# Hybrid encoder block on one core: copies of the meta tokens split before the transposes, another order of a pair's products, weights' parts first when few are ready

## The chip, the cores and the metric

One core of a Trainium2 chip runs one launch of the kernel. The metric is the device time of a launch in microseconds (us). Before the change three runs gave 1146.08, 1146.79 and 1147.39 us; the median is 1146.79 us.

## What is computed

One layer of an encoder on 272 tokens (256 tokens and 16 meta tokens) with 2048 features, all in fp32. The reference, cut to what matters:

```python
hn = rmsnorm(h, mix_norm_g)
q_a, k_a, v_a, cq, ckv, k_pe = split(hn @ w_in)             # 8 heads of 128; ranks 512, 256; 64
out_a = neighbourhood_attention(rmsnorm(q_a), rmsnorm(k_a), v_a, rpb, meta_bias)     # "NA"
q  = rmsnorm(rmsnorm(cq) @ w_q_up)                          # 8 heads of 128 + 64 (rotary)
k, v = split(rmsnorm(ckv) @ w_kv_up)                        # 8 heads of 128 each; k joined with k_pe
out_b = softmax(rope(q) @ rope(rmsnorm(k)).T * scale) @ v   # "MLA"
h = h + concat([rmsnorm(out_a), rmsnorm(out_b)]) @ w_out
h = h + (silu(conv3(hn2 @ w_gate)) * (hn2 @ w_up)) @ w_down # hn2 = rmsnorm(h); 2048 -> 5632 -> 2048
```

## The kernel before

**Three products for one.** Each fp32 operand is split into a high part in the format fp32r (a copy by ScalarE, ACT) and a low part, operand minus high part (a subtraction by VectorE, DVE). A product is hi·hi + hi·lo + lo·hi: three matmuls of a 128x128 block of weights with some 260 columns of tokens (`mm3`, lines 381 to 383), or two in the MLP (`mm2`, lines 1407 and 1408). Nearly all time of TensorE (PE) goes there.

**Weights.** They come in pieces of up to 1024 columns in the order of the list `pieces` (lines 295 to 314). SP loads a piece into one of 5 buffers `raw`; ACT makes `whi` from it (`split_hi`, line 339) and DVE `wlo` (`split_lo`, line 348), 512 columns at a time, into 3 buffers each. PE uses the pieces strictly in order and frees them (`used`). Below, such a half piece of 512 columns in `whi` or `wlo` is a weights' part.

**Attention, by pairs of heads.** After the first projections (cq, ckv, the rotary key) there are four pairs (line 1308). A pair has six stages on PE, in this order: NA queries; the MLA products by `w_q_up` (queries), then by `w_kv_up` (keys and values; `up`, line 1270); NA keys; NA values. What ACT, DVE and POOL (GpSimd) do with the results runs beside the next stages: norms, scores, softmax (`na_tile`, `mla_tile`, `na_small`, `mla_small`), the transposes of the probabilities `p`, and the product with the values (`attend`, line 754).

**The copies of the meta tokens.** The 272 keys are two chunks of 128 and one of 16. For the last chunk all three products are made in one matmul: `p` and the values hold the 16 columns three times, 32 columns apart, behind column 272. In `normalized` (line 739) one DVE instruction scales columns 0 to 255 of `p`, another writes the scaled last 16 columns three times (48 columns). The transposes (`chunks_transposed`, line 719) turn 128, 128 and 80 columns into a PSUM bank. `split_chunks` (line 728) then makes on ACT the high part of the first two chunks, on DVE their low part, on ACT the high part of the third (80 rows), and on DVE the low part of 16 rows of it (`split_last`, line 734). After that the bank is free again; there are two banks for transposes.

**What sets the order.** The kernel is written as generators; a planner, `Flow` (line 83), runs them at build time. A generator asks for an engine with a cost in ns; of those that are ready `run` takes the one with the earliest start, then the lowest `prio`, then the first made. The order of each engine's instructions is fixed by this; on the chip the engines only wait for each other's semaphores. Attention work has `prio` 0, PE's main line 1, the splits of the weights 2 (line 1439). `TO_PE`, 700 ns, is put between another engine's result and PE's use of it.

The two lines that set the choice before:

```python
start = max(self.clock[eng], th.t + self.latency(th, eng))
key = (start, th.prio, th.seq)
```

Of the kernel before, what the change touches and what calls it, by code (L numbers as in the profile page):

```python
# [9 lines left out]
F32 = mybir.dt.float32  # L10
# [32 lines left out]


# [3 lines left out]
LP = L + 3 * CW  # L48
# [32 lines left out]


class Flow:
# [94 lines left out]
def encoder_block(ctx: ExitStack, tc: tile.TileContext, io):  # L178
# [61 lines left out]
    def cost(l, r):  # L240
# [3 lines left out]
        return 0.422 * n + 2 if n >= 256 else max(0.84 * n, 1.67 * m, 27)  # L244
# [53 lines left out]
    for i in range(3):  # L298
        add(io["w_in"][i])
    for pr in range(4):  # L300
# [37 lines left out]

    def split_hi():
        for p in pieces:  # L340
            yield p.loaded
            p.hi = yield from one(his)
            for j, ev in enumerate(p.half):
                a, b = 512 * j, min(512 * j + 512, p.n)
                yield from ACT(p.hi[:, a:b], p.raw[:, a:b], AF.Copy)
                fl.set(ev)

    def split_lo():
        for p in pieces:
            p.lo = yield from one(los)  # L350
            for j, ev in enumerate(p.half):
# [5 lines left out]
                fl.set(p.ready[j])  # L357
            fl.put(raws, p.raw)
# [19 lines left out]
    def mm3(ps, xhi, xlo, start, stop):  # L378
        whi, wlo = yield from block()
        yield "pe", 3 * (0.422 * size(xhi) + 2)  # L380
# [338 lines left out]
    def chunks_transposed(t, pt):  # L719

        yield from TR(
            [(pt[:, :P], t[:, :P]), (pt[:, P : 2 * P], t[:, P:SEQ]), last_transposed(t, pt)]
        )

    def last_transposed(t, pt):
        return pt[:KP, 2 * P : 3 * P], t[:, L : L + KP]
# [7 lines left out]
    def split_last(out, src, lo):  # L734
        yield from ACT(out[:KP], src[:KP], AF.Copy)
        e = slice(lo * CW, lo * CW + N_META)
        yield from TT(out[e], src[e], out[e].bitcast(F32), ALU.subtract)

    def normalized(p, w, a, n=P):

        out, src = thrice(p)
        if a < SEQ:
            yield from TS(p[:n, a:SEQ], p[:n, a:SEQ], w, None, ALU.mult)
        yield from TS(out[:n], src[:n], w, None, ALU.mult)

    def p_transposed(p, PT, q0):
# [4 lines left out]
        yield from split_chunks(PT[:, :, q0 : q0 + P], src, 1)  # L751
# [53 lines left out]
    def small_softmax(p, w, a, b):  # L805
# [4 lines left out]
        yield from normalized(p, w[:4, 2:3], a, 4)  # L810
        fl.put(cols, w)

    def split_small(PT, a, pt):

        for c in range(2):
            o = PT[:, c, :, SEQ:NT]
            src = pt[:, : 3 * P].rearrange("p (c q) -> p c q", c=3)[:, :, 2 * c : 2 * c + 2]
            if a == 0:
                yield from split_chunks(o, src, 1)
            else:  # L820
                yield from split_last(o[:, 2], src[:, 2], 1)
# [70 lines left out]
    def na_values(s, c, ps):  # L892
# [3 lines left out]
        yield from TT(vs[:, :SEQ], ps[:, :SEQ], s1[:, :SEQ], ALU.mult)  # L896
        yield from TT(
            thrice(vs)[0], repeated(ps[:, SEQ:L], 3), repeated(s1[:, SEQ:], 3), ALU.mult
        )
        fl.put(acc, ps)  # L900
        pt = yield from one(tps)
# [3 lines left out]
        yield from split_chunks(V, pt[:, : 3 * P].rearrange("p (c d) -> p c d", c=3), 2)  # L905
# [3 lines left out]
    def na_tile(s, c, i, B, PT, done):  # L909
# [18 lines left out]
        yield from normalized(p, w[:, 2:3], 0)  # L928
        fl.put(cols, w)
        yield from p_transposed(p, PT[:, c], q0)  # L930
        fl.set(done)

    def na_small(s, pr, PT, done):
# [19 lines left out]
        yield from TR([last_transposed(p, pt)])  # L953
# [148 lines left out]
    def mla_tile(s, c, i, PT, done):  # L1102
# [19 lines left out]
        yield from normalized(p, w[:, 2:3], 0)  # L1122
        fl.put(cols, w)
        yield from p_transposed(p, PT[:, c], q0)
# [136 lines left out]
    def attention_weights():  # L1261
# [8 lines left out]
        def up(pr):  # L1270
            s = mla_pair(pr)
# [317 lines left out]
```

## Time and profile before

| | |
|---|---|
| runs before (us) | 1146.08, 1146.79, 1147.39 |
| the profiled execution (us) | 1147.3 |
| its span, first to last instruction (us) | 1145.3 |
| PE busy | 1130.8 us (99%), 8072 matmuls |
| DVE busy | 826.2 us (72%), 1777 instructions |
| ACT busy | 659.1 us (58%), 1466 instructions |
| POOL busy | 118.3 us (10%), 158 instructions |
| first projections and the pairs | to about 291 us of the span, the last pair's rest to 313 us |
| output projection | about 291 to 395 us; then the MLP to the end |

Times of the trace count from the span's first instruction. A matmul's record is longer than the step to the next one (its end is modelled, and matmuls overlap), so that idle time before a matmul is shorter than what is lost. A row of a timeline is: start, duration, engine, line, operation, output<-inputs by the program's names, shapes, count; in brackets the idle time of the engine before it and what ended it. A row of a group is: line, engine, operation, names, shapes, count | busy us, mean ns of one | idle us of the engine before them and what ended it.

### The profile page before, as it was taken

The page shows a single profiled execution, that of the slowest core. Times are in us where ns is not written, and L with a number is a line of the kernel's source. Part 1 is how long each engine was busy: PE and PEld are TensorE (multiplying, and loading weights), DVE is VectorE, ACT ScalarE, POOL GpSimd, SP SyncE. Part 2 cuts the span into 40 slices and gives each one's busy share as a digit, 9 for nine tenths or more (in the row PEclk, how much of TensorE's full clock was granted, in tenths as well). Part 3 has the DMA queues.
Part 4 walks back from the last instruction along what each step waited for, and adds up shares of the span by engine and source line. Part 5 has one row for each costly group of instructions (what it writes and reads, how often), then busy time and mean ns, then how long its engine had stood idle before and what let it go on. Part 6 is the DMA issues. An engine that isn't in the chain of part 4 may idle for free.

```text
span 1145.3 us, 21863 instructions
## 1 busy us (share of the span) xinstructions
PE 1130.8 (99%) x8072; PEld 1064.0 (93%) x8072; DVE 826.2 (72%) x1777; ACT 659.1 (58%) x1466; POOL 118.3 (10%) x158
## 2 busy tenths in 40 slices
PE   8999999999899999999999999999999999999998
PEld 8999999999899999999999999999999888888888
DVE  8779898989977867677667767776777655555553
ACT  7677877878645655555555555555555544444442
POOL 0010202020133510001001000100010000000000
PEclk9999999999999999999999999999999999999999
DMA  9544434443465556555555555555556566766662
GB/s 315 187 137 135 139 120 149 135 152 130 146 196 177 184 180 198 188 188 180 188 186 185 184 185 188 180 190 186 190 178 193 173 193 208 209 198 193 199 195 74
DMA packets 63059, 203.62 MB, mean 178 GB/s; under 512 B 6888, under 2 KB 13416, under 8 KB 62952
## 3 DMA queue, kind: packets, MB, share of 16 engines
q1 hardware_dynamic: 62808, 202.11, 54.9%
q8 instruction: 63, 1.03, 0.4%
q14 instruction: 44, 0.36, 0.1%
q10 hardware_dynamic: 144, 0.12, 0.0%
HBM read 200.10 MB, written 2.10 MB: 177 GB/s over the span
## 4 chain that ended last, share of the span: by engine, by line
PE 87%; DVE 6%; ACT 5%; issue 1%; DMA 1%; POOL 0%; SPq 0%; POOLq 0%; ACTq 0%
PE bank L1407 27%; PE bank L1408 14%; PE bank L383 14%; PE bank L382 14%; PE bank L381 14%; PE bank L250 2%; DVE wlo L214 2%; ACT scr L210 1%; DVE scr L222 1%; ACT whi L210 1%; PE bank L256 1%; ACT bank L210 1%; DVE pt L214 1%; DVE p L218 1%; DMA scr<-in_xT 1%
## 5 line engine op out<-in xcount | busy, mean ns | idle before, releaser
L214 DVE TENSOR_TENSOR wlo<-raw,whi 128x512 fp32r<-128x512 f32 (+1 forms) x737 | 519.4, 714 | 251.8 <-ACT whi L210 248.6
L210 ACT ACTIVATE whi<-raw 128x512 fp32r<-128x512 f32 (+1 forms) x737 | 458.8, 629 | 393.6 <-PE bank L1407 174.7
L381 PE MATMUL bank<-hl,whi 128*128 128x258 f32 (+1 forms) x1232 | 356.8, 290 | 1.8 <-ACT whi L210 1.6
L383 PE MATMUL bank<-hl,wlo 128*128 128x258 f32 (+1 forms) x1232 | 350.6, 285 | 3.6 <-DVE wlo L214 3.6
L382 PE MATMUL bank<-hl,whi 128*128 128x258 f32 (+1 forms) x1232 | 351.1, 285 | 0.0
L1407 PE MATMUL bank<-hl,whi 128*128 128x512 f32 x704 | 246.3, 392 | 0.0
L383 PEld LDWEIGHTS bank<-hl,wlo 128*128 128x128 f32 x1232 | 235.1, 191 | 5.2 <-DVE wlo L214 5.1
L381 PEld LDWEIGHTS bank<-hl,whi 128*128 128x128 f32 x1232 | 232.8, 189 | 4.0 <-ACT whi L210 2.9
L382 PEld LDWEIGHTS bank<-hl,whi 128*128 128x128 f32 x1232 | 234.3, 190 | 0.2
L1407 PE MATMUL bank<-act,whi 128*128 128x512 f32 x660 | 228.8, 391 | 0.0
L1408 PE MATMUL bank<-hl,wlo 128*128 128x256 f32 x704 | 197.5, 281 | 0.0
L1408 PE MATMUL bank<-act,wlo 128*128 128x256 f32 x660 | 184.8, 280 | 0.0
L1407 PEld LDWEIGHTS bank<-hl,whi 128*128 128x128 f32 x704 | 132.0, 188 | 28.9
L1407 PEld LDWEIGHTS bank<-act,whi 128*128 128x128 f32 x660 | 123.4, 187 | 27.1
L1408 PEld LDWEIGHTS bank<-hl,wlo 128*128 128x128 f32 x704 | 132.7, 188 | 0.0
L1408 PEld LDWEIGHTS bank<-act,wlo 128*128 128x128 f32 x660 | 124.7, 189 | 0.0
L238 POOL TENSOR_TENSOR mt<-mt,s 128x256 f32<-128x256 f32 x44 | 41.6, 966 | 459.5 <-ACT mt L210 459.5
L222 DVE SCALAR_TENSOR_TENSOR mt<-mt,vecs,mt 128x256 f32<-128x256 f32 x88 | 40.3, 479 | 0.0
L210 ACT ACTIVATE pt<-bank 128x256 fp32r<-128x256 f32 (+3 forms) x88 | 23.7, 281 | 27.1 <-DVE pt L214 20.0
L381 PE MATMUL bank<-ob,whi 128*128 128x258 f32 x128 | 36.7, 286 | 0.0
L382 PE MATMUL bank<-ob,whi 128*128 128x258 f32 x128 | 36.4, 285 | 0.0
L210 ACT ACTIVATE scr<-scr 128x272 f32<-128x272 f32 x77 | 32.0, 424 | 7.4 <-DVE scr L222 6.3
(216 smaller groups left out, 1220.5 us busy)
## 6 DMA issues: line engine op xcount, KB each, us to landing
raw<-in_w_gate SPq DMA_DIRECT2D x88, 512.0 KB, 4.2
raw<-in_w_up SPq DMA_DIRECT2D x88, 512.0 KB, 4.3
raw<-in_w_down SPq DMA_DIRECT2D x80, 512.0 KB, 4.4
raw<-in_w_in SPq DMA_DIRECT2D x54, 512.0 KB, 4.3
raw<-in_w_out SPq DMA_DIRECT2D x32, 512.0 KB, 4.2
raw<-in_w_down SPq DMA_DIRECT2D x16, 256.0 KB, 3.4
raw<-in_w_cq SPq DMA_DIRECT2D x7, 512.0 KB, 5.9
bias<-in_na_bias SPq DMA_DIRECT2D x8, 272.0 KB, 4.0
```

What stands on the lines that cost most here:

```text
L210: nc.scalar.activation(out, in_, f, **kw)
L214: nc.vector.tensor_tensor(out, a, b, op)
L218: nc.vector.tensor_scalar(out, a, s0, s1, *ops)
L222: nc.vector.scalar_tensor_tensor(out, a, s, b, op0, op1)
L238: nc.gpsimd.tensor_tensor(out, a, b, op)
L250: nc.tensor.matmul(o, l, r, start=start, stop=stop)
L256: nc.tensor.transpose(o, i, ident[:n, :n])
L381: nc.tensor.matmul(ps, whi, xhi, start=start, stop=False)
L382: nc.tensor.matmul(ps, whi, xlo, start=False, stop=False)
L383: nc.tensor.matmul(ps, wlo, xhi, start=False, stop=stop)
L1407: nc.tensor.matmul(ps, whi, x, start=start, stop=False)
L1408: nc.tensor.matmul(ps[:, :n], wlo, x[:, 0, :], start=False, stop=stop)
```

## The change

1. **Copies.** `normalized` and `thrice` go. `p` is scaled in one instruction (272 columns), and the values likewise. The new `meta_copies` copies the 16 columns twice on ACT (32 columns, as high parts) and makes the low part by a subtraction on POOL (16 columns), ahead of the transposes. The third transpose takes 128 columns. `split_chunks` makes the high part of all three chunks in one ACT instruction of 384 columns, and on DVE the low part of the first two; the subtraction of 16 rows on DVE is gone.
2. **Order of a pair's stages**: `ORDER = "QKqkVv"` (capitals MLA, small letters NA). The pieces follow it: `w_kv_up` is loaded as two pieces of 512 columns.
3. **Weights' parts**: `prio` of `split_hi` and `split_lo` is -1 instead of 2 while, after the first 16 pieces, fewer than two pieces beyond PE's place have been split.
4. Costs of matmuls in the planner are larger (0.445 ns a column and 3 for 0.422 and 2; `mm2` 347 for 325). A small copy in `small_sums` goes from POOL to DVE.

```diff
+ORDER = "QKqkVv"
-LP = L + 3 * CW
+LP = L + P
...
-        if th.eng == eng and (eng == "pe" or th.prio >= 2):
+        if th.eng == eng and (eng == "pe" or callable(th.prio) or th.prio >= 2):
...
-                key = (start, th.prio, th.seq)
+                key = (start, th.order(), th.seq)
...
-        return 0.422 * n + 2 if n >= 256 else max(0.84 * n, 1.67 * m, 27)
+        return 0.445 * n + 3 if n >= 256 else max(0.84 * n, 0.84 * m, 27)
...
-    def thrice(row):
+    def meta_copies(row, lo, n=P):
 
-        out = row[:, L : L + 3 * CW].rearrange("p (i x) -> p i x", i=3)[:, :, :N_META]
-        return out, repeated(row[:, SEQ:L], 3)
+        out = row[:n, L : L + 3 * CW].rearrange("p (i x) -> p i x", i=3)[:, :, :N_META]
+        src = row[:n, SEQ:L]
+        his = out[:, :2] if lo == 2 else out[:, ::2]
+        yield from ACT(his.bitcast(F32R), repeated(src, 2), AF.Copy)
+        yield from PTT(out[:, lo].bitcast(F32R), src, out[:, 0], ALU.subtract)
...
     for pr in range(4):
-        for i in range(6):
-            if i == 2:
+        for stage in ORDER:
+            if stage == "Q":
                 add(io["w_q_up"][pr])
-                add(io["w_kv_up"][pr])
-            add(io["w_in"][3 + 6 * pr + i])
+            elif stage in "KV":
+                o = 512 * (stage == "V")
+                add(io["w_kv_up"][pr][:, o : o + 512])
+            else:
+                add(io["w_in"][n_in])
+                add(io["w_in"][n_in + 1])
+                n_in += 2
...
-    def split_chunks(out, src, lo):
+    def split_chunks(out, src):
 
-        yield from ACT(out[:, 0:2], src[:, 0:2], AF.Copy)
+        yield from ACT(out[:, 0:3], src, AF.Copy)
         yield from TT(out[:, 3:5], src[:, 0:2], out[:, 0:2].bitcast(F32), ALU.subtract)
-        yield from split_last(out[:, 2], src[:, 2], lo)
...
-        yield "pool", 150
-        nc.gpsimd.tensor_copy(r[:, 0, : 4 * n], f[:, : 4 * n])
+        yield from COPY(r[:, 0, : 4 * n], f[:, : 4 * n])
...
-        yield from TT(vs[:, :SEQ], ps[:, :SEQ], s1[:, :SEQ], ALU.mult)
-        yield from TT(
-            thrice(vs)[0], repeated(ps[:, SEQ:L], 3), repeated(s1[:, SEQ:], 3), ALU.mult
-        )
+        yield from TT(vs[:, :L], ps[:, :L], s1, ALU.mult)
         fl.put(acc, ps)
+        yield from meta_copies(vs, 2)
...
-        yield from normalized(p, w[:, 2:3], 0)
+        yield from TS(p[:, :L], p[:, :L], w[:, 2:3], None, ALU.mult)
         fl.put(cols, w)
+        yield from meta_copies(p, 1)
         yield from p_transposed(p, PT[:, c], q0)
...
-    for th in (split_x(), split_hi(), split_lo()):
-        fl.spawn(th, 2)
+    fl.spawn(split_x(), 2)
+    fl.spawn(split_hi(), lambda: -1 if 16 < n_split[0] < at[0] + 2 else 2)
+    fl.spawn(split_lo(), lambda: -1 if 16 < n_split[1] < at[0] + 2 else 2)
```

`up` becomes `up_queries`, `up_keys` and `up_values`, which the loop over the pairs calls in the order of `ORDER`. On PE the first 243 rows of the order stand as before, and so do all from the norm of group A (`sum_a`, about 317 us of the span) to the end; between the two the order is another.

**DVE, first pair, at the border from the MLA keys to the next projection** (`wlo` is a weights' part; `late`, `mqr`, `kr`, `mkp` and `scr` belong to MLA's queries and keys, `mv` to its values). Before:

```order
L214 TENSOR_TENSOR wlo_88<-raw_84,whi_85 128x512
L222 SCALAR_TENSOR_TENSOR scr_138<-scr_137,scr_138 128x272
L214 TENSOR_TENSOR mv<-bank_72,mv 128x512
L222 SCALAR_TENSOR_TENSOR scr_133<-scr_138,scr_133 128x272
L214 TENSOR_TENSOR mqr_216<-scr_135,mqr_216 64x258
L222 SCALAR_TENSOR_TENSOR scr_132<-scr_132,gains,scr_133 128x272
L214 TENSOR_TENSOR late_118<-scr_130,late_118 128x272
L214 TENSOR_TENSOR mqr_216<-scr_135,mqr_216 64x258
L214 TENSOR_TENSOR late_117<-scr_132,late_117 128x272
L214 TENSOR_TENSOR mv<-bank_74,mv 16x256
L214 TENSOR_TENSOR scr_133<-kr,scr_133 128x272
L222 SCALAR_TENSOR_TENSOR v_187<-cols_171,emc_c 128x4
```

and now:

```order
L219 TENSOR_TENSOR wlo_89<-raw_82,whi_86 128x512
L227 SCALAR_TENSOR_TENSOR v_186<-cols_170,emc_c 128x4
L219 TENSOR_TENSOR late_117<-scr_132,late_117 128x272
L227 SCALAR_TENSOR_TENSOR v_186<-bank_76,emc_s 4x1
L219 TENSOR_TENSOR mqr_216<-scr_134,mqr_216 64x258
L219 TENSOR_TENSOR scr_138<-kr,scr_138 128x272
L227 SCALAR_TENSOR_TENSOR scr_135<-bank_77,sqx 128x272
L227 SCALAR_TENSOR_TENSOR cols_170<-v_186,cols_170 128x6
L219 TENSOR_TENSOR wlo_90<-raw_83,whi_87 128x512 x2
```

Before, 13 instructions stand between a weights' part and the next (two more follow the rows shown); now it is 7.

**POOL, first pair, the softmax tiles** (`p` are the probabilities, `sq8r` and `qs` belong to the few last queries). Before there is no instruction on `p`:

```order
L238 TENSOR_TENSOR scr_135<-scr_134,consts 128x258
L784 COPY qs_160<-mq_215 128x2x2 x2
L238 TENSOR_TENSOR scr_135<-scr_135,scr_131 128x258
L791 CAST sq8r_164<-sq_162 128x8
L238 TENSOR_TENSOR sq8r_164<-sq_162,sq8r_164 128x8
L1026 COPY qs_160<-mqr_216 128x2x2
L238 TENSOR_TENSOR sum_b<-sum_b,scr_133 128x258
```

and now:

```order
L243 TENSOR_TENSOR sq8r_163<-sq_161,sq8r_163 128x8
L1028 COPY qs_159<-mqr_216 128x2x2
L243 TENSOR_TENSOR p_139<-p_139 128x16
L243 TENSOR_TENSOR p_140<-p_140 128x16
L787 COPY qs_160<-naq_210 128x2x2 x2
L243 TENSOR_TENSOR sq8r_164<-sq_162,sq8r_164 128x4
L243 TENSOR_TENSOR p_141<-p_141 128x16
```

Each set of transposes now has a subtraction of POOL ahead of it, 48 in all (32 tiles of softmax, 8 sets of few queries, 8 of values).

**PE, behind the last projection of the last pair** (`ob` are MLA's outputs, so these are products of the output projection; `consts,p` are transposes, `pt,mv` is `attend` of MLA). Before:

```order
L383 MATMUL bank_75<-ob_204,wlo_90 128x258
L256 MATMUL bank_79<-consts,p_140 128x128 x2
L256 MATMUL bank_79<-consts,p_140 80x128
L256 MATMUL bank_78<-consts,p_141 128x128 x2
L256 MATMUL bank_78<-consts,p_141 80x128
L250 MATMUL bank_76<-pt_157,mv 128x258 x7
L381 MATMUL bank_73<-ob_206,whi_87 128x258
```

and now:

```order
L261 MATMUL bank_79<-consts,p_139 128x128 x3
L255 MATMUL bank_77<-nak_211,qs_160 4x16 x3
L255 MATMUL bank_77<-nak_212,qs_160 4x16 x3
L399 MATMUL bank_74<-ob_194,whi_87 128x258
L400 MATMUL bank_74<-ob_194,whi_87 128x258
L401 MATMUL bank_74<-ob_194,wlo_90 128x258
L255 MATMUL bank_76<-sum_b,consts 128x258
```

Before, both `attend` of the last MLA pair stand among the products of the output projection; now they stand ahead of the end of the last projection, and only NA's transposes and `attend` are left behind it.

## Rows read from the trace of the kernel before

**Rows 1.** The core's span and granted clock; busy time of each engine.

```profile
core 0: 1145.3 us, clock 1.000
...
PE 1130.8 (99%) x8072; PEld 1064.0 (93%) x8072; DVE 826.2 (72%) x1777; ACT 659.1 (58%) x1466; POOL 118.3 (10%) x158
```

**Rows 2.** What PE waited for from 20 to 320 us: total, times, longest.

```profile
PE bank L383 <- DVE wlo L214: 3.2, 5, 0.9
PE bank L256 <- DVE pt L214: 2.3, 3, 1.0
PE bank L256 <- DVE nav L214: 1.1, 1, 1.1
PE bank L250 <- POOL sum_b L238: 0.8, 1, 0.8
PE bank L250 <- DVE pt L214: 0.3, 1, 0.3
```

**Rows 3.** Timeline of PE around the wait at 82.8 us.

```profile
81.64 0.28 PE L382 MATMUL bank<-hl,whi 128*128 128x272 f32 x1
82.82 0.40 PE L383 MATMUL bank<-hl,wlo 128*128 128x272 f32 x1 [0.90 <-DVE wlo L214]
83.06 0.29 PE L381 MATMUL bank<-hl,whi 128*128 128x272 f32 x1
83.18 0.29 PE L382 MATMUL bank<-hl,whi 128*128 128x272 f32 x1
```

**Rows 4.** Stretches: length, busy PE, PEld, DVE, ACT, POOL (instructions), clock, DMA, GB/s.

```profile
269.00:298.00 29.00, 29.00 (x241) 28.57 (x241) 28.30 (x89) 21.48 (x63) 0.00 (x0) 1.00 0.39 128
298.00:320.00 22.00, 18.25 (x139) 16.69 (x138) 19.44 (x44) 11.68 (x35) 7.50 (x8) 1.00 0.69 218
```

**Rows 5.** Timeline of PE: two of the waits for `pt` and `nav`.

```profile
181.97 0.44 PE L256 MATMUL bank<-consts,p 128*128 128x128 f32 x2 [0.74 <-DVE pt L214]
...
299.98 0.55 PE L256 MATMUL bank<-consts,p 128*128 128x128 f32 x3 [1.07 <-DVE nav L214]
```

**Rows 6.** Timeline of DVE at 300 us.

```profile
299.63 0.29 DVE L214 TENSOR_TENSOR nav<-bank,nav 16x128 fp32r<-16x128 f32 x1
```

**Rows 7.** Groups of DVE from 20 to 320 us, by shape.

```profile
L218 DVE TENSOR_SCALAR p<-p,cols 128x256 f32<-128x256 f32 x32 | 11.6, 376 | 0.0
L214 DVE TENSOR_TENSOR pt<-bank,pt 16x128 fp32r<-16x128 f32 x32 | 8.9, 283 | 1.8 <-ACT pt L210 1.0
L218 DVE TENSOR_SCALAR p<-p,cols 128x48 f32<-128x48 f32 x32 | 8.0, 261 | 0.1
```

**Rows 8.** Groups of ACT from 20 to 320 us, by shape.

```profile
L210 ACT ACTIVATE scr<-scr 128x272 f32<-128x272 f32 x68 | 28.2, 424 | 6.5 <-DVE scr L222 6.3
L210 ACT ACTIVATE sq<-qraw 128x4 f32<-128x4 f32 x8 | 1.8, 221 | 0.2
```

**Rows 9.** Groups of PE from 20 to 320 us, by shape: transposes of `p`.

```profile
L256 PE MATMUL bank<-consts,p 128*128 128x128 f32 x88 | 16.8, 276 | 2.9 <-DVE pt L214 1.8 <-DVE nav L214 1.1
L256 PE MATMUL bank<-consts,p 128*80 128x128 f32 x48 | 13.2, 275 | 0.5 <-DVE pt L214 0.5
```

**Rows 10.** Timeline of all engines at 89 us: one tile's scaling and its transposes.

```profile
88.89 0.24 DVE L218 TENSOR_SCALAR p<-p,cols 128x48 f32<-128x48 f32 x1
...
89.58 0.49 PE L256 MATMUL bank<-consts,p 128*128 128x128 f32 x3
```

**Rows 11.** POOL's instructions on `sq8r`: duration in ns, least/median/most.

```profile
L791 POOL CAST sq8r<-sq x8: 183/198/729, 68.0 to 261.1; 128x4 fp32r<-128x4 f32 x4, 128x8 fp32r<-128x8 f32 x4
L238 POOL TENSOR_TENSOR sq8r<-sq,sq8r x8: 203/204/547, 68.3 to 261.4; 128x4 fp32r<-128x4 f32 x4, 128x8 fp32r<-128x8 f32 x4
```

**Rows 12.** Timeline of POOL at 364 us: two adds of one kind.

```profile
364.31 2.74 POOL L238 TENSOR_TENSOR kr<-kr,scr 128x258 f32<-128x258 f32 x1 [3.04 <-ACT scr L210]
...
367.13 0.74 POOL L238 TENSOR_TENSOR kr<-kr,scr 128x258 f32<-128x258 f32 x1
```

**Rows 13.** Timeline of DVE at 364 us.

```profile
364.55 1.90 DVE L214 TENSOR_TENSOR wlo<-raw,whi 128x512 fp32r<-128x512 f32 x3
```

More of the change, by code (lines that the diff above doesn't have):

```diff
@@ L80, in __init__, with order @@
         self.gen, self.t, self.eng, self.prio, self.seq, self.req = gen, t, None, prio, seq, None
+    def order(self):
+        return self.prio() if callable(self.prio) else self.prio
 class Flow:
@@ L346, in split_hi @@
                 fl.set(ev)
+            n_split[0] += 1
     def split_lo():
@@ L719, in chunks_transposed, with row_chunk @@
     def chunks_transposed(t, pt):
-        yield from TR(
-            [(pt[:, :P], t[:, :P]), (pt[:, P : 2 * P], t[:, P:SEQ]), last_transposed(t, pt)]
-        )
-    def last_transposed(t, pt):
-        return pt[:KP, 2 * P : 3 * P], t[:, L : L + KP]
-    def split_chunks(out, src, lo):
-        yield from ACT(out[:, 0:2], src[:, 0:2], AF.Copy)
-        yield from TT(out[:, 3:5], src[:, 0:2], out[:, 0:2].bitcast(F32), ALU.subtract)
-        yield from split_last(out[:, 2], src[:, 2], lo)
[L734 to L744, printed above, removed]
+        yield from TR([(pt[:, j * P : (j + 1) * P], row_chunk(t, j)) for j in range(3)])
+    def row_chunk(t, j):
+        return t[:, L : L + P] if j == 2 else t[:, j * P : (j + 1) * P]
+    def split_chunks(out, src):
+        yield from ACT(out[:, 0:3], src, AF.Copy)
+        yield from TT(out[:, 3:5], src[:, 0:2], out[:, 0:2].bitcast(F32), ALU.subtract)
     def p_transposed(p, PT, q0):
@@ L818, in split_small @@
             if a == 0:
-                yield from split_chunks(o, src, 1)
+                yield from split_chunks(o, src)
             else:
-                yield from split_last(o[:, 2], src[:, 2], 1)
+                yield from ACT(o[:, 2], src[:, 2], AF.Copy)
     def split_query(s, c, q):
@@ L952, in na_small @@
         pt = yield from one(tps)
-        yield from TR([last_transposed(p, pt)])
+        yield from TR([(pt[:, 2 * P : 3 * P], row_chunk(p, 2))])
         fl.put(probs, p)
@@ L1303, in up @@
                 used()
-            fl.spawn(mla_values(s, pss))
-            for c in range(2):
-                fl.spawn(mla_head(s, pr, c))
+            fl.spawn(mla_values(m, pss))
         for pr in range(4):
-            s = na_pair(pr)
-            for c in range(2):
-                fl.spawn(na_head(s, pr, c))
-            pss = yield from project(2, NT)
-            fl.spawn(na_queries(s, pss))
-            yield from up(pr)
-            pss = yield from project(2, L)
-            for c in range(2):
-                fl.spawn(na_keys(s, c, pss[c]))
-            pss = yield from project(2, L)
-            for c in range(2):
-                fl.spawn(na_values(s, c, pss[c]))
+            s, m = na_pair(pr), mla_pair(pr)
+            started = False
+            for stage in ORDER:
+                if stage in "QKV":
+                    if stage == "Q":
+                        for c in range(2):
+                            fl.spawn(mla_head(m, pr, c))
+                    yield from {"Q": up_queries, "K": up_keys, "V": up_values}[stage](m)
+                    continue
+                if not started:
+                    started = True
+                    for c in range(2):
+                        fl.spawn(na_head(s, pr, c))
+                pss = yield from project(2, NT if stage == "q" else L)
+                if stage == "q":
+                    fl.spawn(na_queries(s, pss))
+                for c in range(2):
+                    if stage == "k":
+                        fl.spawn(na_keys(s, c, pss[c]))
+                    elif stage == "v":
+                        fl.spawn(na_values(s, c, pss[c]))
         fl.spawn(load_residual())
@@ L1485, in _layout @@
     for pr in range(4):
-        for base in (0, A, 2 * A):
+        for stage in ORDER:
+            if stage not in "qkv":
+                continue
+            base = A * "qkv".index(stage)
             cols.append(w[:, base + pr * 256 : base + (pr + 1) * 256])
```

28 lines of the change are left out of this document (17 added, 11 removed).

## The prediction

> **What bounds the kernel now.** First the shares: the clock is full (1.000) and PE is busy for 1130.8 of the span's 1145.3 us [rows 1]. Work on PE is not what the change removes, so that the question is what PE loses and where. The waits answer it: between 20 and 320 us PE waited 11 times for another engine, 3.2 + 2.3 + 1.1 + 0.8 + 0.3 = 7.7 us in all [rows 2]. A wait costs more than its idle time: around the one at 82.8 us three steps between starts take 83.18 - 81.64 = 1.54 us, where an undisturbed step is 0.12 us (the last of the four rows), so 1.54 - 0.36 = 1.18 us are lost for 0.90 us of idle time [rows 3]. I take 0.27 us more for each wait: 7.7 + 11 x 0.27 = 10.7 us. That is the most that can be regained here. What comes after the norm of group A, and the first 243 rows of PE, stand in the same order as before, so that nothing is moved there.
>
> Who makes PE wait is read from the stretches: from 269 to 298 us DVE is busy for 28.3 of 29 us, and from 298 to 320 us for 19.4 of 22, while PE falls to 18.3 of 22 [rows 4]. DVE is the second bound in the pairs. Five of the 11 waits are for a weights' part (`wlo`); five are for `pt` or `nav`, that is for a bank to be read out. For one of these the reader can see which instruction ended it: PE goes on at 299.98 us (the second of [rows 5]), and DVE ends the low part of 16 rows of `nav` at 299.63 + 0.29 = 299.92 us [rows 6]. That kind of instruction is one that the change removes.
>
> The profiled execution took 1147.3 us, 2.0 us more than its span; the median of the runs is 1146.8, half a microsecond less. The sum is made against 1147.3 and then moved by this half.
>
> **The change part by part.**
>
> *Copies, on DVE.* For each of 32 tiles of softmax a scaling of 256 columns (376 ns) and one of 48 (261 ns) become one of 272 columns: 376 + 16 x (376 - 261)/208 = 385 ns. That saves 32 x (637 - 385) = 8.1 us by mean durations. The 32 subtractions of 16 rows, 8.9 us, go altogether [rows 7]. Together 17 us, 4.2 us for a pair. The values' and the few queries' own instructions of this kind go too, and eight small copies come from POOL; what is left of that is on the saving side and I count it at nothing. So DVE gets some 4 us of slack in each pair. On PE's path that is worth only what the waits show.
>
> *Copies, on ACT.* The high parts of 80 rows go; the instruction for two chunks grows to three. The 48 new copies of 32 columns have no row: the bounds are 221 ns (4 columns) and 424 ns (272 columns) [rows 8], and I take 240, nearest to the small one. Growth by 128 columns: (424 - 221)/268 x 128 = 97 ns. For 40 large and 48 small ones: 40 x 0.10 + 48 x 0.24 = 15.5 us in 300, before what the removed parts give back. ACT has idle time for it (21.5 of 29 us busy [rows 4]): nothing on the path by itself.
>
> *Copies, on PE.* A transpose to 128 rows takes 276 ns, one to 80 rows 275 [rows 9]: nothing.
>
> *Copies, the chain.* This is where the change adds a wait. Before, DVE's scaling was followed by the transposes directly; now ACT's copy and POOL's subtraction stand between, 48 times. In the one place shown, DVE ends at 89.13 us and PE begins at 89.58, so that 0.45 us of margin remain [rows 10]; it comes from the planner's 700 ns ahead of PE. The planner puts the two new steps into the chain, so the margin itself stays, and only what they take beyond their planned costs counts (133 ns for 16 columns by `PTT`). The nearest rows on POOL, 4 and 8 columns, have a median of 204 ns and a longest of 547; the casts there reach 729 [rows 11]. So a set of transposes is late by nothing (0.07 us is within the margin) in the usual case, and by up to 0.73 - 0.13 - 0.45 = 0.15 us, with 0.27 for the wait, 0.4 us, in a bad one. Bounds for 48: 0 and 19 us. I take one set in ten, where a margin is used up: 5 x 0.4 = 2.0 us. Behind a waiting subtraction on POOL stand the sums of `attend` and the rotary products; PE needs those much later.
>
> *Weights' parts.* The five waits for `wlo` cost 3.2 + 5 x 0.27 = 4.5 us [rows 2]. In the order before, 13 instructions of DVE stand between a part and the next where the wait at 82.8 us falls; now 7. Elsewhere up to 15 still stand between two parts (18 before, twice). I count three quarters as regained: 3.4 us. What is late next is the attention work that is pushed back; DVE's new slack of 4 us a pair covers it, and without that cover it would come back as waits for `pt`.
>
> *Banks and the end of the last pair.* The five waits for `pt` and `nav` cost 2.3 + 1.1 + 0.3 + 5 x 0.27 = 5.0 us, and the wait for POOL's `sum_b` 0.8 + 0.27 = 1.1 us [rows 2]. All but the one at 181.97 us [rows 5] lie from 298 us on, behind the last projection. The instructions that ended them are gone, and MLA's `attend` stands ahead of that point, so that DVE has only NA's tiles left there. I count 4.0 and 0.6 us as regained.
>
> *The rest.* `w_kv_up` in halves: four more issues on SP's queue, and the DMA engines are busy for 0.39 of a stretch in the pairs [rows 4]; hidden. A half piece holds a buffer for half the work of PE, and two follow each other (the second piece of `w_q_up`, then the keys'): PE needs 2 x 12 x 0.12 = 2.9 us for both, enough for a part on ACT and DVE; should it not be, it would show as `wlo` waits and is in the quarter that I left. The loads of `bias` are issued a stage or two later; the scores that need them come after the keys' stage, 96 matmuls of 0.12 us, which covers them. The planner's costs change orders only.
>
> Sum: 3.4 + 4.0 + 0.6 - 2.0 = 6.0 us. 1147.3 - 6.0 = 1141.3, and with the half microsecond 1140.8 us.
>
> **The rivals.**
>
> *All of it.* DVE's slack removes every wait and POOL adds none: 1146.8 - 10.7 = 1136.1 us. For it speaks that DVE is what ends ten of the eleven waits; against it, that a fixed order with planned costs never fits everywhere. 0.08.
>
> *The end stays late.* NA's softmax of the last pair still starts only with the last projection, so that PE catches up with it among the output projection as before. Then the five waits from 298 us on stay (2.3 - 0.74 = 1.5 us of `pt`, the one at 181.97 us taken out [rows 2, 5]; 1.1, 0.8 and 0.3 us; 3.7 + 5 x 0.27 = 5.0 us), and of 10.7 us only the others can go. By the sum: 3.4 for `wlo` and 1.0 for the one wait for `pt` earlier, less 2.0: 1144.4 us. For it: NA's four sets of transposes stand in the new order still behind the last projection. 0.17.
>
> *Moved, not removed.* A weights' part first means an attention instruction later; PE's order has the transposes at a planned place, so that it waits there instead. The same time within 1.5 us of 1146.8. For it: DVE at 28.3 of 29 us [rows 4]; against it: the removed 17 us. 0.12.
>
> *POOL is slower than the waits that go.* An add on POOL was in progress for 2.74 us at 364 us [rows 12], while DVE ran three subtractions of weights' parts without a gap, 1.90 us [rows 13]; the next add of the same kind takes 0.74 [rows 12]. So POOL can be held up by a run of DVE's instructions, and the new order makes more runs of weights' parts. If each of the 48 sets then waits 0.3 us on PE (half of POOL's long rows, with its restart), 48 x 0.3 = 14.4 us come in for 8.0 that go: 1146.8 + 6.4 = 1153.2 us, slower. It decides from 8.0/48 = 0.17 us a set on. Against it: most of POOL's rows are short (medians of 198 and 204 ns [rows 11]). 0.08.
>
> By the Trainium skill ("SBUF — State Buffer", section "Who interferes with whom") a DVE instruction with two inputs in SBUF and a GpSimd instruction that reads SBUF share a port, and the second to come is blocked until the first has ended. The trace agrees in the place named, 2.74 against 0.74 us. Were it to hold at every set, the time would be that of this rival.
>
> **How the numbers follow.** 0.55 for the forecast, 1140.8 us, with a spread of its own from 1138.5 to 1143.5 (the waits regained by more or less of a quarter). 0.2% of 1146.8 is 2.3 us, about what a measurement of this kernel can tell from no change. Faster than 1144.5: the forecast, all of it, and half of the late end, 0.55 + 0.08 + 0.09 = 0.72. Within 2.3 us: the other half and most of the moved waits, 0.08 + 0.10 = 0.18. Slower: POOL and the rest of the moved waits, 0.08 + 0.02 = 0.10. The range reaches from 1136.0, where nothing is left to gain, to 1147.0, where the waits are merely moved; outside it are POOL's rival and about half of the moved waits and of "all of it", under 0.2.
>
> **What would show it.** Right: in the stretch from 20 to 320 us waits for `wlo` fall from 3.2 us to under 1, those for `pt` and `nav` from 3.7 us to under 1; DVE is busy for some 4 us less in a pair; POOL's 48 subtractions have a median near 0.2 us; a new wait of PE for POOL's `p` stays below 2 us. After the norm of group A nothing differs. Wrong: PE waiting for POOL's `p` over 5 us, or a time from 298 to 320 us as long as before for as much work.

## The result and the profile after

The change takes 1134.07 us (median of 4 runs, 1133.82 to 1134.49), the kernel before beside it 1146.88 us: a ratio of 0.9889 [0.9872, 0.9906]. The forecast was 1140.8 us with a range from 1136.0; the direction was right, the gain twice what was forecast, and the time is below the range.

The changed kernel's core row and busy times, against [rows 1]:

```profile
core 0: 1132.2 us, clock 1.000
...
PE 1125.6 (99%) x8072; PEld 1062.2 (94%) x8072; DVE 809.8 (72%) x1685; ACT 660.4 (58%) x1466; POOL 122.4 (11%) x198
```

All that PE waited for from 20 to 320 us (total, times, longest), against the five rows of [rows 2]:

```profile
PE bank L255 <- POOL sq8r L243: 0.3, 1, 0.3
```

The eleven waits are gone; one of another kind, 0.3 us, has come. The same stretches as [rows 4], in the same columns, and then the whole from 20 to 320 us, of the change:

```profile
269.00:298.00 29.00, 29.00 (x243) 28.73 (x242) 26.64 (x65) 23.30 (x66) 6.46 (x12) 1.00 0.66 212
298.00:320.00 22.00, 22.00 (x183) 21.95 (x182) 15.35 (x24) 10.62 (x20) 6.63 (x8) 1.00 0.52 166
...
20.00:320.00 300.00, 299.37 (x2457) 294.66 (x2456) 253.56 (x640) 234.74 (x696) 56.59 (x110) 1.00 0.49 158
```

and the last of these for the kernel before:

```profile
20.00:320.00 300.00, 292.25 (x2362) 284.01 (x2361) 262.63 (x719) 226.41 (x687) 37.79 (x66) 1.00 0.46 150
```

From 298 to 320 us PE is now busy for 22.0 of 22 us (18.25 before). In the whole stretch it starts 95 more matmuls; 95 of 0.12 us are 11.4 us.

To compare kernels where waits are too short for the view, I added up from PE's records what each step from one start to the next takes beyond the usual step of its kind (median; a transpose at 109 ns). This "lost" time is 16.65 us from 20 to 320 us before and 5.32 after; up to 20 us it is 4.89 and 3.71, and from 320 to 410 us 0.37 and -0.15. Together that makes 11.33 + 1.18 + 0.52 = 13.0 of the span's 13.1 us. In all traces the first 20 us lose between 3.5 and 4.9 us, in no order that follows the edits, so that a microsecond there belongs to the single execution; the pairs are where the change works.

### The profile page after: what moved, and what is told of

Same layout as the page of the kernel before. It is cut to its first block, busy times and chain, and to the rows that moved or that the text cites. A ratio compares the mean times of both kernels' runs of the same rounds, so it can differ in the third digit from the quotient of the medians.

```text
span 1132.2 us, 21901 instructions
## 1 busy us (share of the span) xinstructions
PE 1125.6 (99%) x8072; PEld 1062.2 (94%) x8072; DVE 809.8 (72%) x1685; ACT 660.4 (58%) x1466; POOL 122.4 (11%) x198
## 4 chain that ended last, share of the span: by engine, by line
PE 96%; ACT 2%; DMA 0%; DVE 0%; SPq 0%; POOL 0%; issue 0%; POOLq 0%; ACTq 0%
PE bank L1421 28%; PE bank L399 16%; PE bank L400 16%; PE bank L401 16%; PE bank L1422 14%; PE bank L255 4%; PE bank L261 2%; ACT whi L215 1%; ACT scr L215 1%; DMA raw<-in_w_cq 0%; ACT bank L215 0%; SPq L337 0%; ACT mq L215 0%; DVE scr L227 0%; POOL sq8r L243 0%
## 5 line engine op out<-in xcount | busy, mean ns | idle before, releaser
L219 DVE TENSOR_TENSOR wlo<-raw,whi 128x512 fp32r<-128x512 f32 (+1 forms) x737 | 512.9, 705 | 265.3 <-ACT whi L215 262.5
L401 PE MATMUL bank<-ob,wlo 128*128 128x258 f32 x128 | 36.1, 282 | 0.0
```

Source lines behind the costliest of these rows:

```text
L219: nc.vector.tensor_tensor(out, a, b, op)
L401: nc.tensor.matmul(ps, wlo, xhi, start=False, stop=stop)
```

## The experiments

The first theory was the prediction's: DVE has less to do, and what waited for it waits no more. The rivals: a bank of PSUM no longer waits for an instruction that comes late on DVE; or the order, planned with costs that are wrong, now fits. In the table PE's lost time is worked out from each trace as above. The time in us is the median of the runs, but for the first two rows; the lost time is that of the profiled run.

| kernel | us | ratio to before, 95% | PE lost, 20 to 320 us |
|---|---|---|---|
| before (profiled run) | 1147.3 | | 16.65 |
| the change (profiled run) | 1134.06 | | 5.32 |
| after_again | 1134.49 | 0.9894 [0.9879, 0.9909] | 5.47 |
| copies_alone | 1139.06 | 0.9929 [0.9914, 0.9944] | 9.08 |
| order_alone | 1140.12 | 0.9937 [0.9921, 0.9954] | 10.34 |
| first_alone | 1150.03 | 1.0027 [1.0017, 1.0037] | 19.50 |
| costs_alone | 1149.97 | 1.0026 [1.0016, 1.0036] | 20.41 |
| no_copies | 1144.83 | 0.9984 [0.9975, 0.9993] | 15.15 |
| no_order | 1140.66 | 0.9947 [0.9931, 0.9964] | 11.74 |
| no_first | 1136.75 | 0.9912 [0.9897, 0.9927] | 7.21 |
| no_costs | 1137.07 | 0.9916 [0.9901, 0.9931] | 7.46 |
| copies_order | 1136.78 | 0.9914 [0.9897, 0.9930] | 7.31 |
| pool_plus | 1140.77 | 0.9949 [0.9934, 0.9964] | 11.72 |
| dve_load | 1134.24 | 0.9892 [0.9877, 0.9907] | 5.11 |
| off_cheap | 1135.93 | 0.9907 [0.9892, 0.9922] | 6.65 |
| held_right | 1138.11 | 0.9932 [0.9917, 0.9947] | 8.87 |
| held_cheap | 1137.37 | 0.9919 [0.9904, 0.9934] | 8.61 |
| before_fit | 1144.22 | 0.9976 [0.9966, 0.9985] | 14.55 |
| two_reads | 1138.03 | 0.9921 [0.9906, 0.9936] | 9.26 |
| two_scales | 1135.02 | 0.9895 [0.9878, 0.9911] | 5.87 |

### One part alone

Each part of the change was put on the kernel before by itself. **copies_alone**: the copies, the transposes and what reads them.

```
-        yield from normalized(p, w[:, 2:3], 0)
+        yield from TS(p[:, :L], p[:, :L], w[:, 2:3], None, ALU.mult)
         fl.put(cols, w)
+        yield from meta_copies(p, 1)
```

> Of the change only the copies of the meta tokens (and the small copy that goes from POOL to DVE); order of the stages, priority of the weights' parts and the planner's costs as before. Theory A, DVE's load is the cause of the waits: the five waits that ended on a 16-row subtraction go (5 us) and most of those for the weights' parts (2 to 4 us): 1138 to 1140 us. Theory B, the order is the cause: the waits only change their place, 1144 to 1147 us. Theory C, the new hop over POOL costs: PE waits for p from POOL, over 1147 us.

**order_alone**: the order of a pair's products, with its loads.

```
+ORDER = "QKqkVv"
...
+            for stage in ORDER:
```

> Of the change only the order of a pair's stages (and of the pieces of the weights). Theory A, DVE's load: DVE has as much to do as before, the waits for pt and nav stay among the output projection or move into the pairs, 1144 to 1147 us. Theory B, the order: the 5 us of waits at the end of the last pair go, 1140 to 1142 us.

**first_alone**: the weights' parts first when few are ready.

```
-    for th in (split_x(), split_hi(), split_lo()):
-        fl.spawn(th, 2)
+    fl.spawn(split_x(), 2)
+    fl.spawn(split_hi(), lambda: -1 if 16 < n_split[0] < at[0] + 2 else 2)
+    fl.spawn(split_lo(), lambda: -1 if 16 < n_split[1] < at[0] + 2 else 2)
```

> Of the change only the priority of the weights' parts when few are split. Theory A, DVE's load: the waits for wlo go (4.5 us) and come back for the larger part as waits for pt and nav, since DVE has no slack: 1145 to 1148 us. Theory B, the parts were merely placed badly: 4 us less, 1142 to 1143 us.

**costs_alone**: PE's planned costs.

```
-        yield "pe", 3 * (0.422 * size(xhi) + 2)
+        yield "pe", 3 * (0.445 * size(xhi) + 3)
...
-        yield "pe", 325
+        yield "pe", 347
```

> Of the change only the planner's costs of matmuls. Theory A, DVE's load: the orders shift a little, within 1.5 us of the kernel before. Theory B, the plan did not fit the chip: with the measured costs PE's instructions stand where their inputs are ready, and 3 us or more of the waits go, 1144 us or less.

Alone, the copies give 8.1 us and the order 7.1, the one in theory A's range and the other in theory B's. The other two cost 2.8 each, which no theory had. What PE waits for shows which part cures what. With the copies alone (20 to 320 us):

```profile
PE bank L386 <- DVE wlo L214: 2.7, 3, 0.9
PE bank L250 <- POOL sum_b L238: 0.8, 1, 0.8
PE bank L384 <- ACT qraw L210: 0.4, 1, 0.4
```

The waits for `pt` and `nav` of [rows 2] are gone. Those for `wlo` fall only from 3.2 to 2.7 us, though theory A wanted most of them gone, so that its range was met by another account. With the order alone it is the other way about, no `wlo` and small waits for banks and rows:

```profile
PE bank L258 <- DVE p L220: 0.8, 2, 0.6
PE bank L258 <- DVE pt L216: 0.6, 2, 0.4
PE bank L252 <- ACT scr L212: 0.6, 1, 0.6
PE bank L389 <- DVE p L216: 0.5, 2, 0.3
PE bank L252 <- DVE nav L216: 0.4, 1, 0.4
```

And the weights' parts first, alone:

```profile
PE bank L253 <- DVE pt L217: 6.1, 3, 2.3
PE bank L259 <- DVE pt L217: 3.0, 2, 1.7
```

Here too no `wlo` is left, but the waits for `pt` are now 9.1 us, where those for `pt` and `nav` were 3.7 before: on the kernel before, this part does what the rival "moved, not removed" said, and more.

### One part undone

The change without one of the four parts (the diffs above, the other way round), and with two parts only.

> The change without the copies of the meta tokens (order, priority and costs as in the change). The copies alone took 8.1 us off the kernel before, the order alone 7.1, each of the two others alone cost 2.8. Theory A, DVE's load: without the copies DVE has no slack and the priority turns waits for weights' parts into waits for pt: 1141 to 1145 us. Theory B, the order does most: 1136 to 1139 us.

> The change with the kernel before's order of stages. Theory A, DVE's load: copies with priority and fitting costs take away nearly all waits, 1135 to 1137 us. Theory B, the order does most: the end of the last pair waits again, 1139 to 1143 us.

> The change without the priority of the weights' parts. If the priority does harm by itself (2.8 us alone), and DVE's slack from copies and order suffices, nothing is lost: 1133 to 1136 us. If it is what removes the waits for wlo (4.5 us in the kernel before), 1137 to 1139 us, with waits for wlo in the pairs.

> The change with the kernel before's costs of matmuls in the planner. Alone the new costs did harm (2.8 us). If a plan that fits the chip is worth something only where DVE has slack, 1136 to 1139 us; if the costs are of no account, 1133 to 1135.5 us.

> Copies and order of the change, without the priority and the new costs. Theory A, DVE's load: with DVE relieved and the end of the last pair spread, most waits are gone, 1135 to 1138 us, and the two others are worth 1 to 4 us on top. If the gains of copies and order simply added (8.1 and 7.1 us), there would be 1132 us, less than the changed kernel takes.

Against the change's 1134.07 us, the copies are worth 10.8 us, the order 6.6, the weights' parts first 2.7 and the costs 3.0. The last two harm alone and help here, and only as a pair: either without the other (1136.75, 1137.07) is no better than neither (1136.78). What a part is worth depends on the others. Added to the order alone, the two cost 4.7 us (1140.12 against 1144.83 of no_copies), and added to the copies alone 1.6 (1139.06 against 1140.66 of no_order). So much of the 10.8 us is harm that they do where the copies are missing: without the two, the copies give 3.3 us on top of the order, and the order 2.3 on top of the copies.

no_copies, no_order, no_costs and copies_order came out in ranges that were named. no_order's account did not: only 0.8 of its 2.5 us of waits lie from 298 us on. no_first lies between its two ranges and has no wait for `wlo`, the only one listed being 0.8 us for ACT's `p`: where the order is new, these waits are gone without the priority. Without the copies there is a wait that the forecast had not thought of:

```profile
PE bank L396 <- DVE p L219: 4.5, 3, 1.6
PE bank L255 <- ACT scr L215: 1.8, 3, 0.6
```

Its place in the first of three pairs, on PE (start, length, line, operation) and then on DVE:

```profile
112.76 0.82 PE L261 MATMUL bank<-consts,p 128*128 128x128 f32 x6
114.83 0.39 PE L396 MATMUL bank<-late,whi 128*128 128x258 f32 x1 [1.25 <-DVE p L219]
```

```profile
113.24 0.76 DVE L219 TENSOR_TENSOR p<-bank,s 128x256 f32<-128x256 f32 x2
113.92 0.74 DVE L219 TENSOR_TENSOR pt<-bank,pt 128x256 fp32r<-128x256 f32 x2
114.58 0.31 DVE L219 TENSOR_TENSOR p<-bank,s 128x48 f32<-128x48 f32 x2
```

PE's next projection goes into a bank that the values' product still occupies. Its 256 columns are read at 113.24 us, but its last 48 only at 114.58, since two other instructions stand between. In the change one instruction of 272 columns reads all:

```profile
111.15 0.44 DVE L219 TENSOR_TENSOR p<-bank,s 128x272 f32<-128x272 f32 x1
```

### DVE's load and POOL's step

**dve_load** puts 48 reductions on DVE that nothing waits for; **pool_plus** issues each subtraction of `meta_copies` three times and tells the planner of one (first and second diff). **after_again** is the change itself once more, beside them.

```
         yield from PTT(out[:, lo].bitcast(F32R), src, out[:, 0], ALU.subtract)
+        fl.spawn(more_load())
+
+    def more_load():
+        yield from RED(spare, em1, ALU.max)
```

```
         yield from PTT(out[:, lo].bitcast(F32R), src, out[:, 0], ALU.subtract)
+        for _ in range(2):
+            nc.gpsimd.tensor_tensor(out[:, lo].bitcast(F32R), src, out[:, 0], ALU.subtract)
```

> The changed kernel once more, unaltered. If what it gained beyond the 10.7 us of listed waits is in the kernel, 1133.5 to 1134.5 us again and a first stretch (0 to 20 us) as in the changed kernel's profile; if a good part of it was the first loads, which land earlier or later from run to run, up to 1135.5 us.

> The changed kernel with work put back on DVE, a reduction of 272 columns for each of the 48 sets (0.35 us each, 17 us in all, planned, nothing waits for it), so that DVE carries about what the change took off it, while the shorter chain and the banks freed earlier stay. Theory A, DVE's load is the cause: 1140 to 1146 us, towards the change without its copies (1144.8). Rival, the cause was the hold of a bank until a 16-row subtraction came round: within 2 us of the changed kernel.

> The changed kernel with POOL's subtraction of each set issued three times; the planner is not told, so that all orders stay as they are, and each set's last part comes some 0.4 us later. As the prediction had it (0.45 us of margin, 0.27 us for a wait): a part of the sets runs out of margin, 2 to 6 us more, 1136 to 1140 us, with waits of PE for p from POOL. If there is no margin at all: 48 x 0.67 = 32 us more. If the margin is larger than thought: within 1 us of the changed kernel.

after_again takes 1134.49 us, within its range. With dve_load DVE is busy for 823.8 us of the execution, 14.0 more than in the change (809.8) and 2.4 less than before (826.2), and the time stays. Its page, and the stretch from 20 to 320 us:

```profile
PE 1125.9 (99%) x8072; PEld 1062.5 (94%) x8072; DVE 823.8 (73%) x1733; ACT 661.8 (58%) x1466; POOL 120.5 (11%) x198
...
20.00:320.00 300.00, 299.57 (x2458) 294.83 (x2457) 267.51 (x688) 235.97 (x697) 54.87 (x110) 1.00 0.49 158
```

So it is not DVE's relief by itself that brings the gain, and my theory that DVE's load is the cause fell. (The reductions run where DVE has room; work that PE waits for is another matter, below.) pool_plus shows that the hop over POOL does lie ahead of PE. Two more subtractions on POOL in each of 48 sets use up the margin and cost 6.7 us, a little over the 2 to 6 that were expected, with a wait that the change doesn't have:

```profile
PE bank L261 <- POOL p L271: 3.9, 7, 1.1
```

### A bank held, or a plan that doesn't fit

Two theories were left: that a bank of PSUM waits for an instruction to come round on DVE, or that the plan has this instruction too cheap. **held_right** and **held_cheap** put the 16-row subtraction back behind each set of transposes, on rows that no product reads, planned at 315 ns for 128 columns (first diff) or at 201 (68 in place of 182). **off_cheap** is dve_load, planned at 237 instead of 351 ns. **before_fit** is the kernel before with the costs of PE, and 114 ns more for DVE's instructions of 16 or 64 rows (second diff).

```
+        e, n = slice(3 * CW, 3 * CW + N_META), size(src) // 3
+        yield "dve", 182 + 1.04 * n
+        nc.vector.tensor_tensor(out[e, 2], src[e, 2], out[e, 2].bitcast(F32), ALU.subtract)
```

```
-        yield "dve", 68 + 1.04 * size(out)
+        yield "dve", 68 + 114 * (out.shape[0] in (16, 64)) + 1.04 * size(out)
```

> The changed kernel, with one subtraction of 16 rows (16x128, and small ones for the few queries) put back behind each of its 48 sets of transposes on DVE, ahead of the point where the bank of PSUM is given back; it writes rows that no product reads. The planner is told 182 + 1.04 ns per column for it (315 ns, the step between starts in the trace of before). If a bank that waits for its turn on DVE is the cause by itself: 1139 us or more, with waits of PE for DVE's `pt` of over 2 us between 20 and 320 us. If a plan that is wrong by 0.1 us per instruction is the cause: 1133 to 1137 us, since the order then allows for it. If neither (it was the planner's old order alone): 1133 to 1136 us here and in the two runs below.

> The same with the planned cost that the kernel before used, 68 + 1.04 ns per column (201 ns): the instruction is in its old place and the plan is again 0.11 us short for each, some 5 us over the pairs. Plan theory: 1137 to 1142 us, over 1.5 us above the run with the right cost, with waits of PE for `pt`, `p` or `nav` of over 1.5 us between 20 and 320 us. Bank theory: as the run with the right cost, both 1139 us or more.

> The changed kernel with 48 reductions of 272 columns on DVE that nothing waits for, as in the earlier run, but planned at 237 ns instead of 351: the plan is short by the same 0.11 us each, off the chain of the banks. Plan theory: 1137 to 1142 us, over 1.5 us above the 1134.2 us of the earlier run with the right cost. Bank theory: 1136 us or less, since no bank is held by them.

> The kernel before with nothing but the planner's costs set right: the change's own costs of PE, and 114 ns more for DVE's subtractions of 16 rows and rotary instructions of 64. Plan theory: 1136 to 1142 us, the waits for `pt` and `nav` mostly gone. Bank theory: 1145 us or more, since the instruction that holds the bank is still there. The change's costs of PE alone gave 1150.0 us.

The instruction back in its place costs 4.0 us when planned at 315 ns and 3.3 at 201. The cheaper plan is no worse, which speaks against the plan theory. But both times lie under the 1139 us of the bank theory as well, and the waits for DVE's `pt` that it named did not come. held_right's listed waits are all for ACT:

```profile
PE bank L255 <- ACT scr L215: 1.1, 3, 0.4
PE bank L399 <- ACT pt L215: 0.6, 2, 0.3
PE bank L255 <- ACT p L215: 0.5, 2, 0.3
```

By the steps of PE its transposes lose no more than the change's (0.5 and 0.6 us). What it loses more than the change lies at products with `scr` (1.9 us) and with `late` (2.5 us).

The reductions planned too cheap cost 1.7 us more than when planned right; this time, 1135.93 us, is in the bank theory's range. But the plan's errors count as well: before_fit is 5.8 us faster than costs_alone, and its 1144.22 us lie between the two theories' ranges. PE's costs set right make the kernel before slower as long as DVE's are wrong. That the two errors made up for each other in the old plan fits this, but DVE's costs corrected alone were not run. With both corrected, 14.55 of 16.65 us are still lost, so these two errors alone don't explain the kernel before.

Then the values' product (**two_reads**) and the softmax's scaling (**two_scales**), each in two instructions again, otherwise the change:

```
-        yield from TT(vs[:, :L], ps[:, :L], s1, ALU.mult)
+        yield from TT(vs[:, :SEQ], ps[:, :SEQ], s1[:, :SEQ], ALU.mult)
+        yield from TT(vs[:, SEQ:L], ps[:, SEQ:L], s1[:, SEQ:], ALU.mult)
```

```
-        yield from TS(p[:, :L], p[:, :L], w[:, 2:3], None, ALU.mult)
+        yield from TS(p[:, :SEQ], p[:, :SEQ], w[:, 2:3], None, ALU.mult)
+        yield from TS(p[:, SEQ:L], p[:, SEQ:L], w[:, 2:3], None, ALU.mult)
```

> The changed kernel, but the values' product with `s1` is two instructions on DVE again (256 columns, then 16), and the projection's bank is given back after the second. Bank theory, for the projection's banks: the plan puts other instructions of DVE between the two, as in the run without the copies (113.24 and 114.58 us there), and PE's next projection waits for the bank: 1137 to 1140 us, with waits of PE for DVE's `p` of over 2 us in three or more places. If it is only the 16-row subtraction that held a bank too long: 1133 to 1135.5 us and no such waits.

> The changed kernel, but the softmax's scaling is two instructions on DVE again (256 columns, then 16) in all 32 tiles. It holds no bank; it puts some 4 us more on DVE and one step of about 0.14 us into each tile's chain ahead of the copies. Bank theory: 1133 to 1135.5 us. If it is the length of the chain on DVE that counts: 1136.5 to 1139 us, with waits of PE for `p`.

Eight more instructions that read a projection's bank cost 4.0 us; 32 more that hold no bank cost 0.95 us, where the change and its repeat differ by 0.4. Both times are in the bank theory's ranges; the place in two_reads was not as expected. PE waits, but for `scr`:

```profile
PE bank L255 <- ACT scr L215: 3.0, 3, 1.0
```

PE's timeline of two_reads in the first of the three places:

```profile
116.75 0.49 PE L261 MATMUL bank<-consts,p 128*128 128x128 f32 x3
118.22 0.70 PE L255 MATMUL bank<-scr,consts 128*128 128x258 f32 x2 [0.99 <-ACT scr L215]
```

and of the change, at the same two products:

```profile
116.26 0.49 PE L261 MATMUL bank<-consts,p 128*128 128x128 f32 x3
116.51 0.37 PE L399 MATMUL bank<-late,whi 128*128 128x272 f32 x1
...
117.56 0.28 PE L401 MATMUL bank<-hl,wlo 128*128 128x258 f32 x1
117.68 0.60 PE L255 MATMUL bank<-scr,consts 128*128 128x258 f32 x2
```

Between them the change has nine matmuls of projections, and two_reads none: in that plan they stand elsewhere. PE comes to the product with `scr` with nothing else to do, and the view names `scr`, which is only the next thing in a fixed order. A bank that comes free later could show in this way, but no run shows that the bank moved the nine matmuls, and one speaks against a need for it. off_cheap holds no bank longer than the change and has the same pattern once, at the second of these places:

```profile
176.33 0.49 PE L261 MATMUL bank<-consts,p 128*128 128x128 f32 x3
177.80 0.70 PE L255 MATMUL bank<-scr,consts 128*128 128x258 f32 x2 [0.98 <-ACT scr L215]
```

By the steps of PE, products with `scr` lose 3.8 us more in two_reads than in the change, nearly all of its 3.94 in three places, and 1.25 more in off_cheap, nearly all of its 1.33 in one. So a plan that tips at this place costs about 1.25 us, and it can tip without a bank held longer.

held_right (8.87), two_reads (9.26) and two_scales (5.87) lose 3.55 + 3.94 + 0.55 = 8.0 us more than the change, no_copies 9.8. This adds up separate runs; it fits that late reads of banks make up most of what the copies give beside the other parts, and does not show it. A bank that is held is seen directly only in no_copies, with its 4.5 us of waits for `p`.

## Why the prediction was wrong

**Where the time is.** Right: PE's waits in the pairs were what could go, the clock stays at 1.000, and nothing but 0.5 us differs after them. The signs named for a right forecast came true: no waits for `wlo`, `pt` or `nav`, a POOL median near 0.2 us, little waiting for POOL. The sizes were wrong.

**The step that failed** is "I count three quarters as regained", with "I count 4.0 and 0.6 us as regained" beside it: 8.0 of the 10.7 us of waits with their restarts. All of them went, and only 0.3 us of another kind came. That is 2.7 us. The rival "all of it", given 0.08, had the outcome that came true; its reason, DVE's slack, is what dve_load speaks against. Nor is the priority of the weights' parts needed for the waits for `wlo`: order_alone and no_first have none without it.

**POOL's term** was too large: 2.0 us forecast. The 48 subtractions on POOL (least, median, longest in ns):

```profile
L243 POOL TENSOR_TENSOR p<-p x48: 207/223/1376, 76.0 to 293.7; 128x16 fp32r<-128x16 f32 x40, 4x16 fp32r<-4x16 f32 x8
```

The median is near the 204 ns of [rows 11], the longest far above its 729. Yet PE lost 0.24 us for POOL's `p`, in two places. The margin that I took for 0.45 us from one place [rows 10] is larger elsewhere: in the place shown below the longest one takes 1.24 us more than its planned 0.13, and PE loses 0.18. pool_plus shows what happens where margins are used up. This term makes 1.8 us.

**"That is the most that can be regained here"** was wrong too, and with it the range's low end of 1136.0 us. The 10.7 us were made of the waits that the view lists. By the steps of PE 11.3 us went from the pairs, net of the 0.2 that POOL brings, so 11.5, or 0.8 more than that: losses too short for the view. Outside the pairs 0.5 us went between 320 and 410 us and 1.2 in the first 20 us, which differ from run to run. 6.0 + 2.7 + 1.8 + 0.8 + 1.7 = 13.0 us.

**The reasons behind the terms.** That DVE's busy time would fall by 17 us was right in size, 16.4 us by the whole execution (826.2 to 809.8): the 32 scalings of 272 columns take 11.5 us where two groups took 11.6 + 8.0 [rows 7], and the 8.9 us are gone.

```profile
L223 DVE TENSOR_SCALAR p<-p,cols 128x272 f32<-128x272 f32 x32 | 11.5, 358 | 1.2
```

But the forecast made this slack the cover for the weights' parts, and dve_load takes 14.0 us of the slack away at no cost. What helped in its place is shown only in part: banks given back late cost 4.5 us of waits in no_copies, which the forecast had only for the waits at the end, and the rest can be the plan that tips. The ACT term was right: 225 ns for a small copy where I took 240, hidden.

```profile
L215 ACT ACTIVATE p<-p 128x32 fp32r<-128x32 f32 x40 | 8.7, 225 | 2.8 <-DVE p L223 2.7
```

**The rivals.** "The end stays late" is refuted by the full 22 us of PE from 298 us on. "Moved, not removed" holds for first_alone, which is even 2.8 us slower, and not for the whole. "POOL is slower" is refuted, though the blocking it rests on is there:

```profile
138.75 1.38 POOL L243 TENSOR_TENSOR p<-p 128x16 fp32r<-128x16 f32 x1 [0.28 <-ACT p L215]
```

```profile
138.40 1.28 DVE L219 TENSOR_TENSOR wlo<-raw,whi 128x512 fp32r<-128x512 f32 x2
139.60 0.43 DVE L219 TENSOR_TENSOR mkp<-scr,mkp 128x272 fp32r<-128x272 f32 x1
```

POOL's subtraction ends at 140.13 us, after all three of DVE's; PE then lost 0.18 us at the transposes behind it. By the Trainium skill ("SBUF — State Buffer", section "Who interferes with whom") POOL is blocked beside a DVE instruction with two inputs in SBUF. The trace agrees in the place shown, and the time doesn't follow from it.

**Open.** The 16-row subtraction takes more from DVE than the 315 ns of held_right (see the last section), so that run still has it too cheap. The same subtraction behind the point where the bank is given back was not run; it would tell the hold of a bank from the instruction's own price on DVE. Nor was any edit run that holds a bank longer and leaves the order as it is, so bank and plan aren't told apart. Why the weights' parts first and PE's costs help only together was not tried further. No run beat the change; after_again agrees with it.

## What to carry to other kernels

Where several engines share a few banks, look for the last instruction that reads a bank and for what stands ahead of it on its engine: here eight small second reads cost 4.0 us, while 48 reductions that nothing waits for were free. Where the order is planned, a small edit can tip it in a far place, so look there before you name a cause. A wait's name is the next thing in the order and need not be its cause. A part of a change that harms alone can help in the whole, and what a part gives depends on the others, so undo parts as well as trying them. And when an upper bound is made from a list of waits, leave room beyond it for what the list leaves out.

## What was not expected of the hardware

A subtraction of 16 rows costs DVE more than its record of 283 ns [rows 7]. Instructions of 128 rows overlap on DVE: of those of 128x256 with an fp32r result, half start 80 ns or more before the one ahead has ended. The 16-row ones, whose rows begin at partition 32 or 64, don't. In the kernel before, the 40 of 16x128 start 31 ns (median) after the end of the one ahead, and the next starts 31 ns after theirs. The instructions around the one of [rows 6] show it:

```profile
298.75 0.85 DVE L214 TENSOR_TENSOR wlo<-raw,whi 128x512 fp32r<-128x512 f32 x1
...
299.95 0.15 DVE L234 RECIPROCAL cols<-cols 4x1 f32<-4x1 f32 x1
```

298.75 + 0.85 = 299.60 us is 0.03 us ahead of the start at 299.63, and that one's end at 299.92 is 0.03 ahead of 299.95. So each takes about 316 ns from start to start and the overlap of 111 ns (80 + 31) that the one ahead loses: by this estimate 0.43 us, where the planner has 0.20. The Trainium skill ("VectorE: DVE Perf Modes", section "Two Vector instructions with no wait between them") says that an instruction starts only when the earlier ones have finished if an input or the output begins in another group of 32 partitions than the last one in the same memory did, and so does the way back. These gaps agree with it.
